# Mixture of experts: rows of 14 experts added behind the last two, all summed in PSUM by identity and one-hot products; the last norm's scale and bias on VectorE

## The chip, the cores and the metric

The kernel runs on one core of a Trainium2 chip, in one launch. Five engines work side by side, each through its own list of instructions: TensorE (PE in the rows, with its weight loads as PEld), VectorE (DVE), ScalarE (ACT), GpSimd (POOL) and SyncE (SP), which here only issues transfers. The metric is device time in microseconds (us), as the median over several runs; a shorter time is better. A trace of one execution gives every instruction's start and length.

## What is computed

A stack of blocks over 512 tokens of 1024 features, in float32. The change is in the mixture of experts, which stands in two layers and is followed each time by a residual and a layer norm:

```python
def moe_ffn(x, w_router, b_router, w_gate, w_up, w_down):
    ...
    _, top_e = lax.top_k(jnp.where(in_grp, biased, NEG), TOP_K)
    w = jnp.take_along_axis(s, top_e, axis=-1)
    w = w / jnp.sum(w, axis=-1, keepdims=True)
    gate = jnp.zeros((n, N_EXPERTS), jnp.float32).at[jnp.arange(n)[:, None], top_e].set(w)
    h = jax.nn.silu(jnp.einsum('nd,edf->nef', xt, w_gate)) * jnp.einsum('nd,edf->nef', xt, w_up)
    h = h * gate[:, :, None].astype(h.dtype)
    return jnp.einsum('nef,efd->nd', h, w_down).reshape(B, S, D)
...
        f = moe_ffn(x, moe_w_router, moe_b_router, moe_w_gate[i], moe_w_up[i], moe_w_down[i])
        x = layer_norm(DN_ALPHA * x + f, ln_g[i, 1], ln_b[i, 1])
```

There are 16 experts, of which each token takes two, with weights that sum to one.

## The kernel before

Tokens lie in four tiles of 128 partitions x 1024 features, `xt[0..3]`. Most products take three passes (`mm3`, L394 to L396): both factors are split into a high and a low half (`split`, L369: a cast on ScalarE, a subtract on VectorE), and the three products of 512 columns are summed in PSUM.

A mixture layer `L0` or `L1` is an object. `route` and `token_weights` find each token's two experts, the slots of each expert's 128 rows (`idx`) and the two weights of each token (`wts`). For expert e, `gather` reads its rows from `xd` in DRAM (an indirect transfer on GpSimd's queue), transposes them on the PE into the PSUM tile `xgt` (L1431) and splits them. `up` makes 24 products into `psh`, then the gated activation; `down` transposes that (`ht`, L1448), makes 12 products into `psy`, copies `psy` to the SBUF (ScalarE, L1456) and scatters the rows to `yd` in DRAM (L1457), two rows for each token. `experts` writes this as a pipeline: the gather of e + 1, `up` of e, `down` of e - 1. Weights come as 1 MB pieces on SP's queue (L334); the queue runs ahead as pages of the SBUF come free.

`overflow` (L1376 to L1421) is a branch for an expert with more than 128 rows; the branch is not taken here. All engines pass through it.

`combine` comes behind it. It loads `yd` in eight pieces of 512 KB (L1487), each held until all 16 scatters have landed, and adds them to `xt`, weighted, on VectorE (`mac`, L1502; in layer 0 one of them on ScalarE and GpSimd, L1499). By tile follow the statistics (L1512, L1513), a root on ScalarE (L1514), Newton steps on VectorE (L428, L430), `normalize` on ScalarE (L1173), and `done`. VectorE's order in this loop is the order of the code; other engines are ordered by the scheduler. In layer 0 `done` is `x4_tile`: transposes into `x4T` (L1654), scale and bias on both engines (L1660, L1662), splits, and 48 products into `n`, 280 columns at a time. In layer 1 it is `finish` (L1978 to L1983): scale and bias (`affine`, L360), on GpSimd for the first tiles, shared by both engines for the last two, and the store of the tile.

## Time and profile before

| | us |
|---|---|
| median of 3 runs | 1924.97 (1920.96 to 1928.03) |
| profiled execution, whole time | 1918.51 |
| its span, first to last instruction | 1916.7 |
| PE busy in the span | 1743.3 (91%) |
| DVE busy | 1221.8 (64%) |
| ACT busy | 874.1 (46%) |
| POOL busy | 173.3 (9%) |
| experts of layer 0, first transposes to last product | 1096.8 to 1255.9 |
| end of layer 0, to the last product of n | 1255.9 to 1318.2 |
| experts of layer 1 | 1706.1 to 1871.8 |
| end of layer 1 | 1871.8 to 1916.7 |

The share of busy time is a mean over stages with different limits. What a stage is worth is read from its own rows: which engine is full there, and which wait ends last.

### The profile page before, as it was taken

The page shows a single profiled execution, that of the slowest core. Times are in us where ns is not written, and L with a number is a line of the kernel's source. Part 1 is how long each engine was busy: PE and PEld are TensorE (multiplying, and loading weights), DVE is VectorE, ACT ScalarE, POOL GpSimd, SP SyncE. Part 2 cuts the span into 40 slices and gives each one's busy share as a digit, 9 for nine tenths or more (in the row PEclk, how much of TensorE's full clock was granted, in tenths as well). Part 3 has the DMA queues.
Part 4 walks back from the last instruction along what each step waited for, and adds up shares of the span by engine and source line. Part 5 has one row for each costly group of instructions (what it writes and reads, how often), then busy time and mean ns, then how long its engine had stood idle before and what let it go on. Part 6 is the DMA issues. An engine that isn't in the chain of part 4 may idle for free.

```text
span 1916.7 us, 27254 instructions
## 1 busy us (share of the span) xinstructions
PE 1743.3 (91%) x10719; PEld 1480.1 (77%) x10719; DVE 1221.8 (64%) x2276; ACT 874.1 (46%) x1397; POOL 173.3 (9%) x140
## 2 busy tenths in 40 slices
PE   8999999899999999999999799949998999859990
PEld 7899877798989988877888578738886777647870
DVE  7855368776555643253347889874337777669985
ACT  4233346433333332243223288843236665628881
POOL 2310000022000000000000122110000000012213
PEclk9999999899999999999999799979898999879995
DMA  5335221242322233212225599752230003539953
GB/s 194 110 110 140 89 88 65 63 160 90 108 89 89 88 135 114 95 66 88 88 88 206 188 325 380 281 217 77 85 136 23 1 12 123 208 126 338 380 224 140
DMA packets 69205, 269.73 MB, mean 141 GB/s; under 512 B 22144, under 2 KB 24720, under 8 KB 44240
## 3 DMA queue, kind: packets, MB, share of 16 engines
q1 hardware_dynamic: 52384, 246.38, 35.9%
q0 software_dynamic: 9216, 16.80, 2.4%
q10 hardware_dynamic: 7472, 4.76, 1.2%
q8 instruction: 85, 1.39, 0.3%
q14 instruction: 48, 0.39, 0.1%
HBM read 249.62 MB, written 30.43 MB: 146 GB/s over the span
## 4 chain that ended last, share of the span: by engine, by line
PE 63%; DVE 6%; ACT 3%; DMA 2%; issue 2%; POOL 0%; SPq 0%; POOLq 0%; DVEq 0%; ACTq 0%
PE mm L396 8%; PE mm L395 8%; PE mm L394 8%; PE psh L395 3%; PE psh L396 3%; PE psh L394 3%; PE tm L394 2%; PE tm L395 2%; PE tm L396 2%; PE npo L1920 2%; PE npt L1908 2%; PE op L395 2%; PE op L394 2%; PE op L396 2%; PE xgt L1431 1%
## 5 line engine op out<-in xcount | busy, mean ns | idle before, releaser
L369 ACT CAST pg<-pg 128x1024 fp32r<-128x1024 f32 (+2 forms) x437 | 427.4, 1007 | 554.1 <-PE mm L395 224.9
L369 DVE TENSOR_TENSOR pg<-pg,pg 128x1024 fp32r<-128x1024 f32 (+2 forms) x437 | 503.0, 1176 | 264.6 <-ACT pg L369 251.4
L396 PE MATMUL mm<-pg,pg 128*128 128x258 f32 (+2 forms) x1504 | 483.0, 322 | 4.0 <-DVE pg L369 4.0
L394 PE MATMUL mm<-pg,pg 128*128 128x258 f32 (+2 forms) x1504 | 484.9, 323 | 1.4 <-ACT pg L888 0.7
L395 PE MATMUL mm<-pg,pg 128*128 128x258 f32 (+2 forms) x1504 | 482.9, 321 | 0.0
L394 PEld LDWEIGHTS mm<-pg,pg 128*128 128x128 f32 x1504 | 287.6, 191 | 28.0 <-ACT pg L886 2.8
L396 PEld LDWEIGHTS mm<-pg,pg 128*128 128x128 f32 x1504 | 286.8, 191 | 24.9 <-DVE pg L369 4.7
L395 PEld LDWEIGHTS mm<-pg,pg 128*128 128x128 f32 x1504 | 287.4, 191 | 21.2 <-issue 0.4
L360 DVE TENSOR_TENSOR pg<-mm,pg 128x256 f32<-128x256 f32 (+3 forms) x138 | 66.2, 510 | 138.8 <-PE mm L396 138.8
L395 PE MATMUL psh<-pg,pg 128*128 128x512 f32 x256 | 106.4, 416 | 2.3 <-DVE pg L369 2.3
L394 PE MATMUL psh<-pg,pg 128*128 128x512 f32 x256 | 101.9, 398 | 0.0
L396 PE MATMUL psh<-pg,pg 128*128 128x512 f32 x256 | 101.3, 396 | 0.0
L394 PE MATMUL tm<-pg,pg 128*128 128x512 f32 x192 | 76.4, 408 | 4.6 <-ACT pg L1145 4.6
L395 PE MATMUL tm<-pg,pg 128*128 128x512 f32 x192 | 77.3, 403 | 1.2 <-DVE pg L369 1.2
L396 PE MATMUL tm<-pg,pg 128*128 128x512 f32 x192 | 76.1, 396 | 0.0
L360 DVE TENSOR_TENSOR pg<-pg,pg 128x512 f32<-128x512 f32 (+12 forms) x103 | 57.1, 575 | 24.9 <-ACT pg L675 10.6
L1892 ACT ACTIVATE pg<-ns,nmx 128x512 f32<-128x512 f32 (+3 forms) x128 | 66.3, 531 | 11.4 <-DVE nmx L1888 7.2
L1888 DVE TENSOR_REDUCE nmx<-ns 128x2 f32<-128x1024 f32 (+3 forms) x48 | 50.1, 1043 | 17.3 <-PE ns L1885 17.1
L360 DVE TENSOR_TENSOR pg<-pg 128x64 f32<-128x64 f32 (+8 forms) x127 | 49.5, 411 | 17.4 <-ACT pg L1033 15.4
L395 PEld LDWEIGHTS psh<-pg,pg 128*128 128x128 f32 x256 | 48.9, 191 | 13.2 <-DVE pg L369 4.4
L1425 POOL DMA_INDIRECT pg<-xd,idx x32 | 38.1, 1189 | 219.2 <-DVE wts L360 122.7
L394 PEld LDWEIGHTS psh<-pg,pg 128*128 128x128 f32 x256 | 48.8, 191 | 11.4
(440 smaller groups left out, 2960.9 us busy)
## 6 DMA issues: line engine op xcount, KB each, us to landing
pg<-in_w_moe_dram SPq DMA_DIRECT2D x96, 1024.0 KB, 10.4
pg<-in_w_up_dram SPq DMA_DIRECT2D x22, 1024.0 KB, 4.8
pg<-in_w_dn_dram SPq DMA_DIRECT2D x11, 1024.0 KB, 4.9
pg<-in_w_g_dram SPq DMA_DIRECT2D x8, 1024.0 KB, 5.5
pg<-in_w_go_dram SPq DMA_DIRECT2D x8, 1024.0 KB, 4.8
pg<-yd SPq DMA_DIRECT2D x16, 512.0 KB, 7.8
pg<-in_w_n_dram SPq DMA_DIRECT2D x8, 1024.0 KB, 6.8
pg<-in_w_no_dram SPq DMA_DIRECT2D x8, 1024.0 KB, 4.8
```

Source lines behind the costliest of these rows:

```text
L360: return (eng or V).tensor_tensor(o, a, b, op=op)
L369: return A.copy(h, src), V.tensor_tensor(l, src, h.bitcast(F32), op=ALU.subtract)
L394: TE.matmul(o, a[0], b[0], start=start, stop=False)
L395: TE.matmul(o, a[0], b[1], start=False, stop=False)
L396: TE.matmul(o, a[1], b[0], start=False, stop=stop)
L1425: ld = G.indirect_dma_start(out=xg, out_offset=None, in_=self.xd, in_offset=bass.IndirectOffsetOnAxis(ap=self.idx[:, e:e + 1], axis=0), bo ...
L1431: TE.transpose(ps[:, k // 4, (k % 4) * P:(k % 4 + 1) * P], xg[:, k * P:(k + 1) * P], ident)
L1888: V.tensor_reduce(mx, sc, axis=AX.X, op=ALU.max, negate=True)
L1892: A.activation(pp[:, r, br], sc[:, r, br], AF.Exp, bias=mx[:, r, br:br + 1], accum_out=se[:, r, br:br + 1])
L1908: TE.transpose(src[:, r, br, c * P:(c + 1) * P], pp[:, r, br, c * P:(c + 1) * P], ident)
L1920: TE.matmul(o_[64 * r:64 * r + 64], vsw[:, c * 512 + br * 256 + g * 64:c * 512 + br * 256 + (g + 1) * 64], pts[r][:, br, c * P:(c + 1) * P ...
```

## The change

Zeros are written once to a small DRAM tile `zd` and copied from there over both layers' `yd` (`zero`, 16 transfers of 512 KB from DRAM to DRAM). The rows of experts 14 and 15 are not scattered any more. ScalarE scales them by their slot's weight as it copies them (`sw`, found in `token_weights` by eight small products), and VectorE writes a one-hot matrix for each of these two experts and each tile (slot against token, `tokf`). `experts` itself loads `yd` when the scatter of expert 13 has landed, in four pieces of 1 MB, and VectorE adds all of them to `xt` ahead of the overflow branch; the branch reloads `xt` and repeats this if it is taken. In `combine` the PE sums three products by tile in PSUM: identity times `xt`, and the one-hots of experts 14 and 15 times their rows (`early`, `last`). The statistics and `normalize` read PSUM. `gather` loses its transposes to `turn`, which stands behind the sixth of eight steps of `up` of the expert before. In the last layer scale and bias are VectorE's, and the last tile goes out in two halves.

```diff
+    zd = dr.tile([P, 1024], F32, tag="zd", name="zd")
+    G.memset(xt[0], 0.0)
+    nc.sync.dma_start(out=zd, in_=xt[0])
...
+            self.tokf = small("tokf", (2,))
+            V.tensor_scalar(self.tokf, psi[:, 14:16], float(2 * S), None, op0=ALU.add)
...
+            w16, tl = small("w16", (2, 4, 3, 2), F16), small("tl", (2, 4, 2))
+            tt(tl, self.oh[:, :, :, 14:], bc(self.wts, 2), ALU.mult)
...
+            for i, (k, t) in enumerate(self.q):
+                TE.matmul(psp[:, :6], self.q[k, t], w16[:, k, t].rearrange("p a e -> p (a e)"), start=i == 0, stop=i == 7)
...
+        def zero(self):
+
+            for i in range(2 * S // P):
+                nc.sync.dma_start(out=self.yd[i * P:(i + 1) * P, :], in_=zd)
+
+        def load(self, t, y):
+            return nc.sync.dma_start(out=v2(y), in_=self.yd.rearrange("(a k) d -> a k d", k=2)[t * P:(t + 1) * P])
+
+        def mac(self, t, y):
+            for k in range(2):
+                V.scalar_tensor_tensor(xt[t], y[:, k * 1024:(k + 1) * 1024], self.wts[:, k, t:t + 1], xt[t], op0=ALU.mult, op1=ALU.add)
...
+        def turn(self, xg, behind=None):
+
             ps = p2("xgt")
             for k in range(KD):
-                TE.transpose(ps[:, k // 4, (k % 4) * P:(k % 4 + 1) * P], xg[:, k * P:(k + 1) * P], ident)
+                i = TE.transpose(ps[:, k // 4, (k % 4) * P:(k % 4 + 1) * P], xg[:, k * P:(k + 1) * P], ident)
+                if behind is not None:
+                    after(i, behind)
...
+            if e < 14:
+                A.copy(v2(yo), psy)
+                s = self.scatter(yo, self.idx[:, 16 + e:17 + e])
...
+            self.last = A.activation(v2(yo), psy, AF.Copy, scale=self.sw[:, e - 14:e - 13]).ins.name
+            m = self.xg[1][:, (e - 14) * 512:(e - 13) * 512]
+            for t in range(4):
+                V.tensor_scalar(m[:, t * P:(t + 1) * P], iota, float(t * P), self.tokf[:, e - 14:e - 13], op0=ALU.add, op1=ALU.is_equal)
+            self.late.append((m, yo))
...
+            xg = {0: self.gather(0)}
+            g, hs = {0: self.turn(xg.pop(0))}, {}
             for e in range(17):
                 if e == 1:
                     wt.behind = None
                 if e < 15:
-                    g[e + 1] = self.gather(e + 1)
+                    xg[e + 1] = self.gather(e + 1)
                 if e < 16:
                     hs[e] = self.up(g.pop(e))
+                if e < 15:
+                    g[e + 1] = self.turn(xg.pop(e + 1), self.upto)
                 if e > 0:
                     self.down(e - 1, hs.pop(e - 1))
-            drop("xg", "gh", "gl", "hs", "hhl", "ysb", "wr", "wh", "wl")
+
+            for t in range(4):
+                y.append(sb(2048, "wr", F32, WM))
+                ld = self.load(t, y[t])
...
+            for t in range(4):
+                self.mac(t, y[t])
...
+            def early(t):
+
+                ps = p2("late")
+                for nh in range(2):
+                    c = slice(nh * 512, (nh + 1) * 512)
+                    TE.matmul(ps[:, nh], ident, xt[t][:, c], start=True, stop=False)
+                    TE.matmul(ps[:, nh], self.late[0][0][:, t * P:(t + 1) * P], self.late[0][1][:, c], start=False, stop=False)
+                return ps
+
+            def last(t):
+                for nh in range(2):
+                    TE.matmul(z[t][:, nh], self.late[1][0][:, t * P:(t + 1) * P], self.late[1][1][:, nh * 512:(nh + 1) * 512], start=False, stop=True)
+
+            z = [early(0), early(1)]
+            last(0)
+            last(1)
...
+                            V.bn_stats(bs[:, 6 * j:6 * j + 6], z[t][:, j])
...
+                        normalize(v2(xt[t]), z[t], rs)
+                    if t in (1, 2):
+                        z.append(early(t + 1))
+                        last(t + 1)
...
     def finish(t):
-        n = (0, 0, 512, 640)[t]
-        for eng, c in ((V, slice(0, n)), (G, slice(n, 1024))):
-            if c.start < c.stop:
-                affine(xt[t][:, c], [g[:, c] for g in L1.gb], eng)
-        nc.sync.dma_start(out=out[t * P:(t + 1) * P, :], in_=xt[t])
-    L1.combine(finish, ())
+        for c in (slice(0, 1024),) if t < 3 else (slice(0, 512), slice(512, 1024)):
+            affine(xt[t][:, c], [g[:, c] for g in L1.gb], V)
+            nc.sync.dma_start(out=out[t * P:(t + 1) * P, c], in_=xt[t][:, c])
+    L1.combine(finish)
```

How the order moves, at three places. First the PE at the start of layer 1's experts, before: `xgt` is a transposed gather, `psh` the first products of expert 0.

```order
L1306 MATMUL inv<-rr,pg_8436 128x32
L1431 MATMUL xgt<-c_ident,pg_132 128x128 x8
L1431 MATMUL xgt<-c_ident,pg_10600 128x128 x8
L1431 MATMUL xgt<-c_ident,pg_7017 128x128 x8
L394 MATMUL psh<-pg_10084,pg_10085 128x512
L395 MATMUL psh<-pg_10084,pg_10085 128x512
L396 MATMUL psh<-pg_10084,pg_10085 128x512
```

And now, at the second gather's transposes, which stand at the end of `psh` of expert 0:

```order
L394 MATMUL psh<-pg_8476,pg_10552 128x512
L395 MATMUL psh<-pg_8476,pg_10552 128x512
L396 MATMUL psh<-pg_8476,pg_10552 128x512
L1474 MATMUL xgt<-c_ident,pg_10672 128x128 x8
L394 MATMUL psh<-pg_10549,pg_10146 128x512
L395 MATMUL psh<-pg_10549,pg_10146 128x512
L1495 MATMUL ht<-c_ident,pg_10817 128x128 x2
```

The transposes of the second and third gather have moved behind products of the expert ahead of them.

Second, VectorE at the end of layer 1's experts, before: the branch of `overflow` (L1376, L1377), with its inner steps, and behind it the additions.

```order
L369 TENSOR_TENSOR pg_13862<-ht,pg_13862 128x256
L1376 TENSOR_LOAD cnti
L1377 COMPARE_AND_BRANCH
L1379 COPY posr<-pos 128x8
L1381 COMPARE_AND_BRANCH
```

```order
L1377 UNCONDITIONAL_BRANCH
L1502 SCALAR_TENSOR_TENSOR pg_7017<-pg_132,wts,pg_7017 128x1024
L1502 SCALAR_TENSOR_TENSOR pg_7017<-pg_7017,wts 128x1024
L1512 BN_STATS bs<-pg_7017 128x6 x2
L1513 BN_AGGR mv<-bs 128x2
L1502 SCALAR_TENSOR_TENSOR pg_132<-pg_7061,wts,pg_132 128x1024
```

And now:

```order
L369 TENSOR_TENSOR pg_11433<-ht,pg_11433 128x256
L1460 SCALAR_TENSOR_TENSOR pg_7017<-pg_92,wts,pg_7017 128x1024 x2
L1460 SCALAR_TENSOR_TENSOR pg_132<-pg_94,wts,pg_132 128x1024 x2
L1460 SCALAR_TENSOR_TENSOR pg_7060<-pg_11460,wts,pg_7060 128x1024 x2
L1460 SCALAR_TENSOR_TENSOR pg_7060<-pg_7094,wts,pg_7060 128x1024 x2
L1395 TENSOR_LOAD cnti
L1396 COMPARE_AND_BRANCH
```

All eight additions have moved ahead of the branch; no addition is left behind it.

Third, the PE behind the branch in layer 0, before: the first tile's transposes `x4T` come first, then the products `n`.

```order
L1377 UNCONDITIONAL_BRANCH
L1654 MATMUL x4T<-c_ident,pg_7017 128x128 x8
L394 MATMUL n_10153<-pg_8465,pg_483 128x280
L1654 MATMUL x4T<-c_ident,pg_132 128x128 x8
L395 MATMUL n_10153<-pg_8450,pg_483 128x280
```

And now, where `late` are the sums in PSUM (L1558 is the identity's product, L1559 and L1564 the one-hots' of experts 14 and 15):

```order
L1559 MATMUL late<-pg_7017,pg_7064 128x512
L1564 MATMUL late<-pg_6402,pg_7064 128x512 x4
L1718 MATMUL x4T<-c_ident,pg_7017 128x128 x8
L394 MATMUL n_10210<-pg_8476,pg_483 128x280
L395 MATMUL n_10210<-pg_8080,pg_483 128x280
L1558 MATMUL late<-pg_7060,c_ident 128x512
L1559 MATMUL late<-pg_7017,pg_7064 128x512
L1558 MATMUL late<-pg_7060,c_ident 128x512
L1559 MATMUL late<-pg_7017,pg_7064 128x512
L1564 MATMUL late<-pg_6402,pg_7064 128x512 x2
L396 MATMUL n_10210<-pg_8476,pg_10145 128x280
```

Twelve products stand ahead of the first transposes (four for each of two tiles and then two for each), and the third tile's six have come in between the first products of `n`; the fourth's stand in the second tile's `n`.

## Rows read from the trace of the kernel before

**Rows 1.** Busy time by stretch: length, engines (x instructions), PE clock, DMA share, GB/s.

```profile
1744.00:1844.00 100.00, 99.49 (x484) 81.73 (x483) 92.69 (x97) 87.02 (x107) 23.57 (x19) 1.00 0.96 370
...
1880.00:1890.00 10.00, 0.00 (x0) 0.00 (x0) 9.20 (x16) 1.83 (x3) 2.04 (x1) 0.50 0.91 345
```

**Rows 2.** VectorE in order of time, layer 1's end: start, length, what; [idle before].

```profile
1880.11 1.28 DVE L1502 SCALAR_TENSOR_TENSOR pg<-pg,wts,pg 128x1024 f32<-128x1024 f32 x1 [11.02 <-DMA pg<-yd]
...
1883.16 1.29 DVE L1512 BATCH_NORM_STATS2 bs<-pg 128x6 f32<-128x512 f32 x2
...
1887.84 1.29 DVE L1512 BATCH_NORM_STATS2 bs<-pg 128x6 f32<-128x512 f32 x2
...
1889.28 2.10 DVE L1502 SCALAR_TENSOR_TENSOR pg<-pg,wts,pg 128x1024 f32<-128x1024 f32 x1
...
1891.54 2.06 DVE L428 SCALAR_TENSOR_TENSOR bs<-lrs,bs 128x1 f32<-128x1 f32 x1
```

**Rows 3.** GpSimd in order of time: expert 13's scatters, and the last norm's end.

```profile
1246.68 1.11 POOL L1457 DMA_INDIRECT yd<-pg,idx  x1 [7.78 <-ACT pg L1456]
...
1862.52 1.11 POOL L1457 DMA_INDIRECT yd<-pg,idx  x1 [7.78 <-ACT pg L1456]
...
1907.07 3.16 POOL L360 TENSOR_TENSOR pg<-pg,pg 128x384 f32<-128x384 f32 x2 [1.75 <-ACT pg L1173]
```

**Rows 4.** Scatters, issue to landing in us: expert 13's in layer 0, layer 1, all.

```profile
yd<-pg,idx POOLq DMA_INDIRECT x1, 3.3
...
yd<-pg,idx POOLq DMA_INDIRECT x1, 6.3
...
yd<-pg,idx POOLq DMA_INDIRECT x32, 8.8
```

**Rows 5.** PE in order of time, layer 0's end.

```profile
1272.57 1.97 PE L1654 MATMUL x4T<-c_ident,pg 128*128 128x128 f32 x8 [16.66 <-ACT pg L1173]
1282.73 0.60 PE L394 MATMUL n<-pg,pg 128*128 128x280 f32 x1 [8.19 <-ACT pg L369]
...
1287.55 0.29 PE L395 MATMUL n<-pg,pg 128*128 128x280 f32 x1
...
1303.35 0.40 PE L394 MATMUL n<-pg,pg 128*128 128x280 f32 x1 [3.17 <-ACT pg L369]
...
1318.22 0.39 PE L394 MATMUL tm<-pg,pg 128*128 128x512 f32 x1
```

**Rows 6.** PE in order of time, around a float32 product of 512 columns (z).

```profile
831.13 1.02 PE L1100 MATMUL z<-pg,pg 128*128 128x512 f32 x2
...
832.23 0.40 PE L395 MATMUL tm<-pg,pg 128*128 128x512 f32 x1
```

**Rows 7.** ScalarE in order of time, layer 1's end.

```profile
1886.64 1.24 ACT L1173 ACTIVATE pg<-pg,lrs 128x1024 f32<-128x1024 f32 x1 [1.62 <-DVE lrs L1520]
```

**Rows 8.** VectorE in order of time, layer 0's end.

```profile
1302.83 0.73 DVE L1662 TENSOR_SCALAR pg<-x4T,lnfm 128x128 f32<-128x128 f32 x2 [1.48 <-ACT pg L1660]
```

**Rows 9.** PE in order of time, the start of both layers' experts.

```profile
1102.39 0.78 PE L394 MATMUL psh<-pg,pg 128*128 128x512 f32 x1
...
1103.27 0.40 PE L396 MATMUL psh<-pg,pg 128*128 128x512 f32 x1
...
1706.14 1.97 PE L1431 MATMUL xgt<-c_ident,pg 128*128 128x128 f32 x8 [5.84 <-DMA pg<-xd,idx]
...
1716.57 0.78 PE L394 MATMUL psh<-pg,pg 128*128 128x512 f32 x1
```

**Rows 10.** VectorE in order of time, the first gather's subtract in layer 0.

```profile
1099.85 1.22 DVE L369 TENSOR_TENSOR pg<-xgt,pg 128x1024 fp32r<-128x1024 f32 x1 [4.12 <-ACT pg L369]
```

**Rows 11.** VectorE in order of time, four one-hots in layer 1's routing.

```profile
1699.17 0.86 DVE L1299 TENSOR_SCALAR pg<-c_iota,pos 128x128 f16<-128x128 f32 x4
```

**Rows 12.** SP's queue in order of time, where the zeros come in.

```profile
794.70 34.46 SPq L334 DMA_DIRECT2D pg<-in_w_gv_dram  x4
```

**Rows 13.** ScalarE in order of time, the first cast of w_gq.

```profile
882.11 1.05 ACT L369 CAST pg<-pg 128x1024 fp32r<-128x1024 f32 x1 [4.46 <-PE tm L396]
```

More of the change, by code (lines that the diff above doesn't have):

```diff
@@ L1438, in up @@
             for k in range(KD):
-                mm3(psh, (g[0][:, k * P:(k + 1) * P], g[1][:, k * P:(k + 1) * P]), wt.next(512), k == 0, k == KD - 1)
+                i = mm3(psh, (g[0][:, k * P:(k + 1) * P], g[1][:, k * P:(k + 1) * P]), wt.next(512), k == 0, k == KD - 1)
+                if k == 5:
+                    self.upto = i.ins.name
             hs = sb(256, "hs", bufs=2)
@@ L1455, in down @@
             yo = sb(1024, "ysb", bufs=3)
-            self.last = A.copy(v2(yo), psy).ins.name
-            s = G.indirect_dma_start(out=self.yd, out_offset=bass.IndirectOffsetOnAxis(ap=self.idx[:, 16 + e:17 + e], axis=0),
-                                     in_=yo, in_offset=None, bounds_check=2 * S - 1, oob_is_err=False)
-            for o in self.scat:
-                tc.declare_no_dep(s.ins, o.ins, reason="rows of another expert's tokens")
-            self.scat.append(s)
+            if e < 14:
+                A.copy(v2(yo), psy)
+                s = self.scatter(yo, self.idx[:, 16 + e:17 + e])
+                for o in self.scat:
+                    tc.declare_no_dep(s.ins, o.ins, reason="rows of another expert's tokens")
+                self.scat.append(s)
+                return
+            self.last = A.activation(v2(yo), psy, AF.Copy, scale=self.sw[:, e - 14:e - 13]).ins.name
[3 more added lines that the diff above has]
+            self.late.append((m, yo))
         def experts(self):
-            drop("zT", "lng", "lnb")
+            drop("zT", "lngb")
             wt.bufs = 4
-            self.scat = []
-            g, hs = {0: self.gather(0)}, {}
+            self.scat, self.late, y = [], [], []
+            xg = {0: self.gather(0)}
+            g, hs = {0: self.turn(xg.pop(0))}, {}
             for e in range(17):
@@ L1491, in combine @@
+            st.behind = ld.ins.name
+            for t in range(4):
+                self.mac(t, y[t])
+            drop("gh", "gl", "hs", "hhl", "wr", "wh", "wl")
+            wt.bufs = 2
+        def combine(self, done):
             self.gb = load_gb(2 * self.l + 1)
-            st.behind = ld.ins.name
             eps = small("epsl", (1,))
             V.memset(eps, LN_EPS / ALPHA ** 2)
-            def mac(t, k):
-                if k == 0 and t in aside:
-                    A.activation(y2[t, 0], y2[t, 0], AF.Copy, scale=self.wts[:, 0, t:t + 1])
-                    tt(xt[t], xt[t], y2[t, 0], ALU.add, G)
-                else:
-                    V.scalar_tensor_tensor(xt[t], y2[t, k], self.wts[:, k, t:t + 1], xt[t], op0=ALU.mult, op1=ALU.add)
+            def early(t):
[11 more added lines that the diff above has]
+            last(1)
@@ L1674, in x4_tile @@
         nc.sync.dma_start(out=kcd[t * P:(t + 1) * P, :], in_=s_)
-    L0.combine(x4_tile, (3,))
+    for _ in range(2):
+        sb(512, "kcv", bufs=2)
+    L0.combine(x4_tile)
     drop("x4f")
```

60 lines of the change are left out of this document (32 added, 28 removed).

## Prediction

> **What bounds the kernel now.** I read four views, in this order. First the busy times by stretch: inside the experts the PE is busy 99.5 of 100 us at full clock, so a mixture layer gains nothing there; what can move is its start and its end, where the PE idles. In the last layer's end the PE does nothing, its clock stands at 0.50, and VectorE is the full engine (9.2 of 10 us) [rows 1]. Second, the order of time on VectorE in that end: the first addition waits 11 us for the load of yd, and then a tile costs 4.7 us while GpSimd is idle (1883.16 to 1887.84); beside GpSimd's scale and bias, an addition of 1.28 us takes 2.10 and a step on a single column 2.06 [rows 2]. Third, GpSimd's and the queues' rows: the scatter of expert 13 starts at 1862.52, 17.6 us before the first addition, since the loads wait for that of expert 15 [rows 2, 3]. Fourth, the PE in the first layer's end: 16.7 us idle before the first transposes, 8.2 before the next norm projection n, 3.2 later, and dense work from there on [rows 5]. So the time ends, in layer 0, when n of the fourth tile is through (1318.22), and in layer 1 with the last store.
>
> **The change part by part.** I call S the landing of expert 13's scatter, M the end of the eight additions, P the start of the first product with the identity.
>
> *End of layer 1.* Expert 13's scatter starts at 1862.52; such scatters land 3.3 to 6.3 us later, so S is 1865.8 to 1868.8, and I take 1867.5 [rows 3, 4]. The four loads are 4.2 MB; at the 345 GB/s of this stretch that is 12.2 us [rows 1], the additions follow as the tiles land, and the last pair is 2.5 us [rows 2]: M = S + 15 = 1882.5. The rows of order show that all eight stand ahead of the branch around the overflow on VectorE, and the PE's first product waits for that branch; so P = 1882.8, not the time of the first tile. The PE has idled since its last expert then and is at 0.50 [rows 1]. A float32 product of 512 columns: z is one, in two records; it starts at 831.13, and the next stream is back at its normal pace at 832.23, whose first step of 0.23 lies before that; so 0.87 us at full clock, 1.74 at half [rows 6]. How long the half clock lasts I take from layer 0, where n began at 0.50 at 1282.73 and ran at the full rate by 1287.5: some 4.4 us [rows 5]. Ten products stand ahead of the first statistics: 2.5 in 4.4 us, 7.5 in 6.5, together 10.9. So the first statistics come at 1893.7, where they now come at 1883.16.
> Then the tiles. Statistics and their sum are 1.5, the steps to the inverse root 0.9 (the 4.7 us of an undisturbed tile, less those 1.5 and two additions of 1.2), its wait for ScalarE's root some 0.3, normalizing 1.24 [rows 2, 7]: the first tile's result leaves PSUM at P + 14.9. There are two such PSUM buffers, so the third tile's six products run from there to P + 20.1, the fourth's to P + 25.3. VectorE then has the fourth statistics (to 26.8), scale and bias of the third tile (two of 1.2, the additions' length: 29.2), Newton (30.1), normalizing on ScalarE (31.4), and four half-width steps of 0.65: P + 34.0. From the last step to the end it is 6.5 us now (GpSimd's end at 1910.2 to 1916.7) [rows 3], less 0.5 allowed for a store of half the size: P + 40 = 1922.8, **+6 us**. What is won from GpSimd (twice 2.7 us of slowed steps) and from the early loads is spent on products at a cold clock and a serial PSUM chain. Bounds: S at its early end and a warm clock -4, -2; the clock falling again in the gap before P + 14.9, and S late, +2, +1.5; with an allowance for waits: 0 to +12.
>
> *End of layer 0.* The same with S = 1250.0 (1246.68 + 3.3) [rows 3, 4]: M 1265, P 1265.5, first statistics 1276.4, first transposes 1280.4, against 1272.57. To the first n it is another 4.6 us: VectorE has the multiply by the scale (1.2), the pair of 0.73, the add and the second pair [rows 8], so n starts at 1285.0 against 1282.73: +2.3. Behind it the PE was 35.5 us at work to 1318.22. Twelve more products lie in that stretch now, 10.4 us; of the waits that they can fill there are 3.17 and the half clock behind it, some 1.7 [rows 5]. I let them fill 4: 2.3 + 10.4 - 4 = 8.7, of which I take **+8** (from +2, all filled and n as early as now, to +13, none filled). What follows is dense PE work, so it is passed on.
>
> *Start of a layer.* In layer 0 the first expert's rows are transposed, cast and subtracted by 1101.1, and psh could start there instead of 1102.39 [rows 9, 10]: -1.3. But the other two gathers' transposes now lie behind psh (2 x 0.87), the second's cast and subtract (1.0 and 1.22, less 0.5 of products that need only the high half) stand open between psh of expert 0 and 1, and the clock, which was full from 1103.3 on because the transposes ran on, is lost for half of another 4.4 us (2.2): -1.3 + 1.7 + 1.7 + 2.2 = 4.3, less 0.7 of waits that were there already; I take **+3** (0 to +5). In layer 1 psh stood behind the third gather until 1716.57; the first transposes end at 1708.1 [rows 9], and with 2.2 for the split and 0.5 allowed for the sw steps ahead of the subtract it moves to 1710.8: -5.8 + 1.7 + 1.7, less 0.7: **-3** (-5 to +1). The clock is at half in both orders there.
>
> *The rest.* Eight one-hots a layer are 0.86 us per four on VectorE [rows 11], which is 93% busy in the experts [rows 1]; ScalarE's copies gain no length: **+1** for both layers (0 to 3.4). The sw products and sums fall in the wait for gathers: 0 (to 1.5). The two scatters less per layer were behind the PE: 0. The zeros are 8.4 MB from DRAM to DRAM, which no row shows. They go between the loads of w_gv and w_gq on SP's queue; w_gv's last issue is at 829.2, w_gq's first cast at 882.1 [rows 12, 13]. With a memset and a store ahead (about 5 us) and w_gq's load behind (about 5), they have 42 us. At the 370 GB/s of the expert loads they take 23, and 46 if each byte counts twice: 0 (to +4); I take 0, since the loads are the nearest row.
>
> Sum: 6 + 8 + 3 - 3 + 1 = **+15 us**. The profiled execution took 1918.5 us (span 1916.7), 6.5 under the median; it would come to 1933.5, the median to **1940**. Half a per cent is 9.6 us, about what a measurement here can tell from no change.
>
> **The rivals.**
> *The products start with the first tile.* If the first product waits only for its own two additions, P is 7.5 us earlier in both layers: the sums at the ends fall to about -1.5 and +0.5, the whole to 0: **1925**, not slower. Against it stands the order of the branch; for it, that the semaphore's count is all that I have. It decides at P: 1875 against 1882.
> *One pass.* If a product of 512 columns costs 0.23 as the experts' do, the first statistics come 6 us sooner and VectorE's 4.8 us a tile becomes the pace: -2 in each end, **1922**. Against it: z's two records [rows 6].
> *Late scatters.* If expert 13's rows land 8.8 us after issue, the median of all scatters [rows 4], S moves by 5.5 in layer 0 and 4 in layer 1: **1949**. Expert 13's own 3.3 and 6.3 speak against it, VectorE's full load for it. The Trainium skill, "SBUF — State Buffer", section "SBUF: two separate sides", states a rule for this: descriptors of GpSimd's transfers can't be written while a VectorE operation holds the port pair that the two share. [...]
> *A cold PE.* If the clock stays at 0.50 in the last norm (the PE waits for buffers), twelve products cost 0.87 more each: **1950**.
> *Zeros in the way.* At 100 GB/s they end near 918, and w_gq is some 40 us late: **1980**. Nothing in the trace speaks for so low a rate.
>
> **How the numbers follow.** Forecast 0.44 (own range 1928 to 1952; 0.10 of it within half a per cent), early start 0.16 (0.12 within, 0.04 faster with the starts at their low ends), one pass 0.08 (0.05 and 0.03), late scatters 0.09 (0.01 within), cold PE 0.09, zeros 0.07, a wait that goes and that I have not priced 0.07 (0.05 faster, 0.02 within). Faster 0.12, within 0.30, slower 0.58. The range 1921 to 1957 leaves out the zeros and most of the faster cases.
>
> **What would show it.** Right: in layer 1 the last addition ends near 1882 and the first product right behind it; records of such products of twice 0.43 us, longer at first; statistics 4.7 to 5.5 us apart; no step of 2 us on VectorE; n of the fourth tile in layer 0 ending some 8 us later against the first transposes of its experts; the PE idle for 2 us behind psh of expert 0. Wrong: a product ahead of the additions' end, tiles closer than 4.7 us, w_gq's first cast waiting for its load, or a PE that is idle in the experts.

## The result and the profile after

The changed kernel takes 1943.64 us (median of 4 runs, 1942.19 to 1946.63), the kernel before in the same comparison 1923.57 (1920.96 to 1928.03). The ratio is 1.0105, with a 95% interval from 1.0084 to 1.0126: slower by 1%, 20 us. Forecast were 1940 us and +15. The direction and the time are as forecast; several terms of the sum are not, and that their misses cancel in part is luck.

Where the time went is read from the PE's own milestones in the two profiled executions (spans 1916.7 and 1941.7): first and last instruction of each stage, one subtracted from the other. (`go` and `op` are products ahead of layer 0's experts, `tm` and `cim` products behind `n`.)

| stage, us | before | after | difference | forecast |
|---|---|---|---|---|
| start to the first `op` products (near 1012) | 1012.2 | 1015.5 | +3.3 | 0 |
| from there to the experts of layer 0 | 84.6 | 85.6 | +1.0 | 0 |
| experts of layer 0, first `xgt` to last `psy` | 159.1 | 163.7 | +4.6 | +3, and half a us of one-hots |
| end of layer 0, last `psy` to the first `cim` | 90.2 | 108.0 | +17.8 | +8 |
| from there to the experts of layer 1 | 360.0 | 361.3 | +1.3 | 0 |
| experts of layer 1 | 165.6 | 161.9 | -3.7 | -3, and half a us of one-hots |
| end of layer 1, last `psy` to the end | 45.0 | 45.7 | +0.7 | +6 |

The sum is +25.0, where the forecast had +15. It is also 5 more than between the medians, which is what the profiled execution of before lies below its own median (1918.51 against 1923.57); the one of after lies on its median. A difference of that size is seen in one stage: layer 0's experts took 159.1 us in that execution, and 164.7 and 165.3 in the two others that have the same order there (below).

Layer 0's end on the PE in order of time (start, length, what, idle before it), to be held against [rows 5]:

```profile
1274.25 2.05 PE L1558 MATMUL late<-pg,c_ident 128*128 128x512 f32 x2 [9.47 <-DVEq L1396]
1276.09 1.91 PE L1559 MATMUL late<-pg,pg 128*128 128x512 f32 x2
...
1281.52 1.02 PE L1559 MATMUL late<-pg,pg 128*128 128x512 f32 x2
...
1291.85 1.97 PE L1718 MATMUL x4T<-c_ident,pg 128*128 128x128 f32 x8 [4.16 <-ACT pg L1177]
...
1297.18 0.60 PE L394 MATMUL n<-pg,pg 128*128 128x280 f32 x1 [3.36 <-ACT pg L369]
...
1297.82 1.91 PE L1558 MATMUL late<-pg,c_ident 128*128 128x512 f32 x2
...
1327.11 0.40 PE L394 MATMUL n<-pg,pg 128*128 128x280 f32 x1 [3.57 <-ACT pg L369]
...
1338.59 0.40 PE L394 MATMUL n<-pg,pg 128*128 128x280 f32 x1 [2.05 <-ACT pg L369]
```

The products wait for VectorE's pass through the branch and start at half clock: a product is two records, and products follow each other 1.71 us apart (1276.09, 1277.80), later, at full clock, 0.86 (1281.52, 1282.38). The first transposes come 27 us after the last expert product, where they came 16.7 after it before, and `n` still waits twice later on.

VectorE in the same stretch:

```profile
1263.89 10.15 DVE L1460 SCALAR_TENSOR_TENSOR pg<-pg,wts,pg 128x1024 f32<-128x1024 f32 x8 [1.75 <-DMA pg<-yd]
...
1285.92 1.91 DVE L369 TENSOR_TENSOR pg<-pg,pg 128x1680 fp32r<-128x1680 f32 x1 [7.12 <-ACT pg L369]
1287.75 1.29 DVE L1574 BATCH_NORM_STATS2 bs<-late 128x6 f32<-128x512 f32 x2
```

All eight additions in one piece, done at 1274.04; M was to be S + 15, and `yd`'s loads were issued at 1259.23: 14.8. Then something that the prediction did not have: the first statistics stand behind a subtract of a piece of `w_n1`, whose cast waits for its transfer.

Layer 1's end on VectorE, to be held against [rows 2]:

```profile
1894.94 5.12 DVE L1460 SCALAR_TENSOR_TENSOR pg<-pg,wts,pg 128x1024 f32<-128x1024 f32 x4 [1.57 <-DMA pg<-yd]
1901.26 5.12 DVE L1460 SCALAR_TENSOR_TENSOR pg<-pg,wts,pg 128x1024 f32<-128x1024 f32 x4 [1.20 <-SPq L1396]
1917.92 1.29 DVE L1574 BATCH_NORM_STATS2 bs<-late 128x6 f32<-128x512 f32 x2 [11.54 <-PE late L1564]
...
1920.59 1.29 DVE L1574 BATCH_NORM_STATS2 bs<-late 128x6 f32<-128x512 f32 x2
...
1925.18 1.29 DVE L1574 BATCH_NORM_STATS2 bs<-late 128x6 f32<-128x512 f32 x2
...
1929.94 1.29 DVE L1574 BATCH_NORM_STATS2 bs<-late 128x6 f32<-128x512 f32 x2
...
1935.92 2.74 DVE L360 TENSOR_TENSOR pg<-pg,pg 128x512 f32<-128x512 f32 x4 [1.33 <-ACT pg L1177]
```

The eight additions end at 1906.38, 10.3 us after the last expert product; VectorE then has nothing to do for 11.5 us. The second tile's statistics follow the first's by 2.7 us, the next ones by 4.6 and 4.8, and no step of 2 us on a single column is left; GpSimd does nothing here.

The PE at the same place, and its granted clock there (columns: length; busy us of PE, PEld, VectorE, ScalarE, GpSimd with instructions; clock; DMA share; GB/s):

```profile
1906.59 2.04 PE L1558 MATMUL late<-pg,c_ident 128*128 128x512 f32 x2 [10.56 <-DVEq L1396]
...
1911.71 1.02 PE L1559 MATMUL late<-pg,pg 128*128 128x512 f32 x2
...
1916.00 3.60 PE L1564 MATMUL late<-pg 128*128 128x512 f32 x8
1919.43 1.02 PE L1558 MATMUL late<-pg,c_ident 128*128 128x512 f32 x2
```

```profile
1905.00:1910.00 5.00, 3.41 (x4) 1.50 (x5) 1.34 (x2) 0.00 (x0) 0.00 (x0) 0.50 0.02 7
1910.00:1915.00 5.00, 5.00 (x11) 2.19 (x10) 0.00 (x0) 0.00 (x0) 0.00 (x0) 0.84 0.00 0
```

Last, a difference that has nothing to do with the change. Between 1000 and 1016 us, where both kernels run the same products, the PE of the changed kernel was busy without a gap at half clock:

```profile
1000.00:1016.00 16.00, 16.00 (x71) 14.95 (x71) 7.35 (x20) 2.22 (x3) 2.41 (x3) 0.51 0.00 1
```

The same stretch of before stands at 1.00. The stage from `go` to `op`, in which it lies, takes 26.08 us here and 19.39 to 19.40 in the profiled executions of before and of all experiments below: 6.7 us in one execution of 14, taken as chance here. (The table's first row has +3.3 and not +6.7, since the first `go` came 3.4 us sooner in after; it lies between 986.5 and 994.1 in the 14 executions.)

### The profile page after: what moved, and what is told of

The parts are those of the page before. It is cut to its first block, busy times and chain, and to the rows that moved or that the text cites. A ratio compares the mean times of both kernels' runs of the same rounds, so it can differ in the third digit from the quotient of the medians.

```text
span 1941.7 us, 27485 instructions
## 1 busy us (share of the span) xinstructions
PE 1796.7 (93%) x10831; PEld 1503.2 (77%) x10831; DVE 1225.0 (63%) x2315; ACT 877.2 (45%) x1396; POOL 145.8 (8%) x128
## 3 DMA queue, kind: packets, MB, share of 16 engines
q1 hardware_dynamic: 52032, 255.30, 36.6%
## 5 line engine op out<-in xcount | busy, mean ns | idle before, releaser
L360 DVE TENSOR_TENSOR pg<-pg,pg 128x512 f32<-128x512 f32 (+11 forms) x109 | 61.5, 584 | 36.9 <-PE x4T L1718 12.4
L1958 ACT ACTIVATE pg<-ns,nmx 128x512 f32<-128x512 f32 (+3 forms) x128 | 66.2, 529 | 10.4 <-DVE nmx L1954 6.0
L394 PEld LDWEIGHTS psh<-pg,pg 128*128 128x128 f32 x256 | 49.3, 193 | 17.4 <-ACT pg L369 7.3
L395 PEld LDWEIGHTS psh<-pg,pg 128*128 128x128 f32 x256 | 49.3, 193 | 13.4 <-DVE pg L369 3.2
L396 PEld LDWEIGHTS psh<-pg,pg 128*128 128x128 f32 x256 | 49.3, 192 | 13.0 <-DVE pg L369 2.8
```

Source lines behind the costliest of these rows:

```text
L360: return (eng or V).tensor_tensor(o, a, b, op=op)
L394: TE.matmul(o, a[0], b[0], start=start, stop=False)
L395: TE.matmul(o, a[0], b[1], start=False, stop=False)
L396: return TE.matmul(o, a[1], b[0], start=False, stop=stop)
L1958: A.activation(pp[:, r, br], sc[:, r, br], AF.Exp, bias=mx[:, r, br:br + 1], accum_out=se[:, r, br:br + 1])
```

## Experiments

The theory after the result: the loss lies in layer 0's end alone; it is made by products that stand between the additions and the statistics on a PE that has gone cold, and by further products in a stretch where the PE sets the time. Layer 1's end pays the same products, but gets their price back from VectorE. The rivals are those of the prediction and the start of the layers.

### One layer's end undone at a time

In `l0_old` layer 0 is as before from its scatters on (all 16 scattered, `combine` as it was), and its zeros and the steps for `sw` are left out too; layer 1 is as changed. In `l1_old` it is the reverse. `turn` keeps its new place in both.

```diff
-    L0.combine(x4_tile)
+    L0.combine_old(x4_tile, (3,))
```

> Layer 0 as before the change from its scatters on (16 scatters, eight loads behind the last one, additions and statistics as before), with the new place of the transposes; layer 1 as changed. Theory: the loss lies in layer 0's end, where the traces show 17.7 us more from the last expert product to the stream behind n; it should go, so some 1926 us, and the end of layer 0 as long as before (90 us from the last psy to cim). Rival: the ends are neutral and the loss lies ahead of them (a stretch of products at half clock near 1000 us, the starts of the experts): then 1941 to 1944, with the end of layer 0 no shorter than 16 us less.

> Layer 1 as before the change from its scatters on, GpSimd sharing scale and bias; layer 0 as changed. Theory: in layer 1 the late first statistics (10 us) and the faster tiles and end (10 us) cancel, so the time stays at 1943, within 2 us. Rival: taking GpSimd out of the last norm is a gain by itself that the products only partly eat: then putting it back costs 4 us or more, 1948. A third possibility, that layer 1's end is a loss: under 1940.

`l0_old`: 1917.9 us, ratio 0.9978 (0.9960 to 0.9996). Its milestones are those of before in layer 0's end (89.2 us against 90.2 before and 108.0 after), and layer 1's end is 44.9. So the whole loss is gone, and a small gain is left. `l1_old`: 1940.78, ratio 1.0084 (1.0064 to 1.0104), with layer 0's end at 108.0 and layer 1's at 44.3: undoing layer 1 takes 1.4 us off its end, and the interval of the ratio overlaps that of the changed kernel (1.0084 to 1.0126). The loss lies in layer 0's end; layer 1's end is neutral to within some 1.5 us.

### The transposes in their old place

```diff
-                    xg[e + 1] = self.gather(e + 1)
+                    g[e + 1] = self.turn(self.gather(e + 1))
...
-                if e < 15:
-                    g[e + 1] = self.turn(xg.pop(e + 1), self.upto)
```

> Only the transposes of a gather go back to their place ahead of the products of the expert before. Theory: in layer 0 the stretch from the first transposes to the last expert product gets 4 to 5 us shorter (no open split between psh of expert 0 and 1, clock up earlier), in layer 1 it gets 3 us longer (third gather waited for): 1942 in all. Rival: the place of the transposes sets the pace of every expert: then both layers move the same way by over 5 us, 1933 or 1953.

1948.78 us, ratio 1.0124 (1.0106 to 1.0142): not shorter but, if anything, longer. The experts take 165.3 us in layer 0 and 166.7 in layer 1, against 163.7 and 161.9 with the new place. The PE at layer 0's start shows why the forecast for layer 0 was wrong:

```profile
1104.52 1.97 PE L1474 MATMUL xgt<-c_ident,pg 128*128 128x128 f32 x8 [4.57 <-DMA pg<-xd,idx]
1106.14 0.78 PE L394 MATMUL psh<-pg,pg 128*128 128x512 f32 x1
```

The third gather's rows come 4.6 us late and hold the first products, as they did in layer 1 before, 10.4 us behind the first transposes there [rows 9]. In the profiled execution of before they happened to be on time in layer 0, and `psh` began 5.6 us after the first transposes. That was taken for the rule. The last gathers of both layers before, layer 0's with the second one in one line:

```profile
1098.95 3.80 PE L1431 MATMUL xgt<-c_ident,pg 128*128 128x128 f32 x16 [0.18 <-DMA pg<-xd,idx]
...
1714.95 1.97 PE L1431 MATMUL xgt<-c_ident,pg 128*128 128x128 f32 x8 [4.51 <-DMA pg<-xd,idx]
```

### The zeros alone

The kernel before, with `zd` and the 16 copies at the place where the change has them.

```diff
+            for i in range(2 * S // P):
+                nc.sync.dma_start(out=self.yd[i * P:(i + 1) * P, :], in_=zd)
```

> The kernel before, with the cleared tile and the 16 copies of zeros added at the place where the change has them, and nothing else. Theory: the copies are hidden; the time is that of before, within 3 us, and the first product with w_gq starts as before. Rival: the copies shift the work of the mixer behind them so that its short products run at half clock near 1000 us, as in the changed kernel: 7 us more, 1930, with a granted clock of 0.5 between 1000 and 1016 us. If half clock shows there in this run and not in others, it is chance and not the copies.

1925.05 us, ratio 0.9999 (0.9986 to 1.0013): hidden. In the changed kernel SyncE issues the 16 copies from 831.75 to 848.1, and the queues are full from 840 to 860 (columns as above):

```profile
820.00:840.00 20.00, 19.66 (x96) 13.66 (x94) 8.96 (x14) 5.24 (x6) 1.42 (x2) 1.00 0.58 207
840.00:860.00 20.00, 17.03 (x73) 13.24 (x71) 11.82 (x15) 14.02 (x10) 0.53 (x1) 1.00 0.97 309
860.00:880.00 20.00, 17.24 (x66) 13.91 (x67) 5.99 (x9) 8.15 (x8) 0.00 (x0) 0.83 0.40 141
```

The start stage of this run (993.2 us up to the first `go`) is that of before (992.8). In the same run the third gather of layer 0 waits 4.4 us and the experts take 164.7: the 159.1 of before's profiled execution is the exception.

### The weight piece ahead of the statistics

`a_wn` is the changed kernel with the piece of `w_n1` that is loaded last split behind the first tile's `x4T` and used last in `n`; the loads of scale and bias go behind it.

```diff
+        if i == 0:
+            mid, st.mark = raw, st.lds[st.used - 1]
...
+        if t == 0:
+            split(mid, *w1[0])
...
-        for k in range(KD):
+        for k in (3, 4, 5, 6, 7, 0, 1, 2):
```

> The changed kernel, with three moves in layer 0's end alone: the piece of w_n1 that is loaded last is split behind the first tile's x4T work and used last in n, and the loads of the norm's scale and bias stand behind it on SP's queue. Theory: the first statistics of layer 0 were held 2.7 us by that split (the products for them had ended at 1285.0, the statistics began at 1287.75); they now follow the products, and from the last psy to cim it is 2.7 us less, 105. Rival: the products behind n set that stretch whatever the statistics do; then 108 stays.

1938.49 us, ratio 1.0066 (1.0045 to 1.0087). VectorE's first statistics now follow the products:

```profile
1281.47 1.29 DVE L1578 BATCH_NORM_STATS2 bs<-late 128x6 f32<-128x512 f32 x2 [7.22 <-PE late L1568]
```

That is 11.7 us behind the first product (1269.77) instead of 13.5, and layer 0's end is 105.6 us instead of 108.0: 1.8 of the 2.4 us at this step of the chain.

### A PE that is kept busy

`warm` lets the PE multiply the identity with itself behind the last expert, 36 products of 128 columns, while the additions run.

```diff
+            ps = p1("warm")
+            for _ in range(36):
+                after(TE.matmul(ps[:, :P], ident, ident, start=True, stop=True), self.fin)
```

> The changed kernel, with 36 idle products (identity by identity, 128 columns, into a PSUM tile that nobody reads) behind the last expert's, in both layers, so that the PE is busy for 8 of the 10 us before its first sum. Theory: the half clock at the start of the sums costs 2.2 us on the path. In layer 1 the first statistics come 2.2 us sooner after the last addition (8.7 instead of 11.3) and the end is 43.5 instead of 45.7; in layer 0 nothing is gained, because the split of w_n1 holds the statistics there. In all 1941. Rival: the clock is not on the path: 45.7 stays. If the clock is at 0.50 all the same, such products don't keep it up.

1940.47 us, ratio 1.0075 (1.0053 to 1.0096). The clock in layer 1's end is full (compare the two rows of after):

```profile
1905.00:1910.00 5.00, 3.92 (x23) 2.80 (x23) 2.84 (x3) 0.00 (x0) 0.00 (x0) 1.00 0.50 185
1910.00:1915.00 5.00, 5.00 (x13) 2.16 (x12) 0.00 (x0) 0.00 (x0) 0.00 (x0) 1.00 0.00 0
```

From the first product to the first statistics it takes 8.9 us (1908.08 to 1916.94) instead of 11.3, and layer 1's end 41.8 instead of 45.7. So the cold clock is worth 2.5 us of the 11.3, and the ten products at full clock are the rest, 8.9. Another 1.4 us of the shorter end are not the clock's: here VectorE's eight additions run without a wait, where they waited 1.2 us in their middle in the changed kernel, and the first product follows the last expert product by 9.1 us instead of 10.6. In layer 0 nothing comes of it (108.3 us): there the weight piece holds the first statistics to 1284.72 all the same, 13.5 us behind the first product.

### Without the identity

`v_add` has the PE sum only the two one-hot products of a tile, and VectorE adds that sum to `xt`. `v_add2` is `v_add` with the moves of `a_wn`. In both, and in the three kernels at the end of this section, the third and fourth tile's products also stand one tile earlier in the code.

```diff
-                    TE.matmul(ps[:, nh], ident, xt[t][:, c], start=True, stop=False)
...
+                        tt(v2(xt[t]), v2(xt[t]), z[t], ALU.add)
```

> The changed kernel without the identity's products: the PE sums only the two one-hot products, which need no addition to be done first, and VectorE adds that sum to xt (one 1024-wide step more for each tile). Theory: the loss is the path from the last addition through ten products at a cold clock, and twelve products behind n. Then in layer 1 the first statistics come some 8 us sooner and the end gets 6 to 8 us shorter (38 instead of 45.7); in layer 0 the stretch from the last psy to cim gets 10 us shorter by the products alone (98), with the first statistics still held by the split of w_n1. In all 1926. Rival: VectorE and the loads set the ends and the products lie beside them: then four more steps of 1.2 us a layer make it 1948.

> v_add with the three moves of a_wn. Theory: the first statistics of layer 0 follow the last addition by one step of 1.2 us; from the last psy to x4T some 15 us instead of 27, to cim some 84 instead of 108; layer 1 as in v_add; in all 1912. Rival: PE work behind n keeps the stretch at 98 as in v_add, since transposes and splits of the next tiles come no sooner: 1926.

`v_add`: 1925.65 us, ratio 0.9994 (0.9980 to 1.0009). By the medians that is 18 us less than the changed kernel, with one product in three gone. The two ends give 12.6 of them (102.0 us instead of 108.0 in layer 0, 39.0 instead of 45.7 in layer 1); the rest lies in neither end, so that the whole came out at the 1926 expected is partly luck. The PE and VectorE of `v_add` in layer 1's end:

```profile
1887.37 3.70 PE L1558 MATMUL late<-pg,pg 128*128 128x512 f32 x8 [1.20 <-ACTq L1396]
1890.91 3.60 PE L1563 MATMUL late<-pg 128*128 128x512 f32 x8
```

```profile
1891.33 5.12 DVE L1460 SCALAR_TENSOR_TENSOR pg<-pg,wts,pg 128x1024 f32<-128x1024 f32 x4 [1.27 <-SPq L1396]
1896.67 1.22 DVE L360 TENSOR_TENSOR pg<-pg,late 128x1024 f32<-128x1024 f32 x1 [0.21 <-DVEq L1396]
1897.92 1.29 DVE L1574 BATCH_NORM_STATS2 bs<-pg 128x6 f32<-128x512 f32 x2
```

The one-hot products need neither `xt` nor the branch's part on VectorE: the PE begins them 1.2 us behind its last expert product, at full clock (1.00 from 1890 to 1900), while VectorE still adds. The sum stands ready when VectorE wants it, and the first statistics come 1.5 us behind the additions instead of 11.5. The end is 39.0 us.

`v_add2` was expected at 1912 and took 1925.61, ratio 1.0004 (0.9985 to 1.0023), as its rival had it. Layer 0's end goes from 102.0 to 98.8 us, but not to the 90.2 of before. Up to the first `n` it is as short as before (26.6 us against 26.8); what is left over lies between the first `n` and the first `cim`: 63.4 us before, 72.2 here. The PE is busy 6.9 us longer in it (with the last tile's four one-hot products, mostly at half clock, and 1.6 us more for the `tm` products) and idles 5.7 us against 3.8: that is the 8.8. The PE is busy 92% of this stretch, and what it is given there is passed on. This last part, about half of layer 0's 17.8 us, is read from the rows: no run takes the one-hot products out of that stretch, or puts the identity last in layer 0.

### The additions behind the branch

The rival of the early start: the eight additions come behind the overflow branch, so that the first product waits for the first tile's pair alone.

```diff
-            for t in range(4):
-                self.mac(t, y[t])
...
+            with tc.manual_schedule(engines={mybir.EngineType.DVE}):
+                for t in range(4):
+                    self.mac(t, self.y[t])
```

> The changed kernel with the eight additions moved behind the overflow branch (the loads stay ahead of it; the branch, if taken, loads yd again). If the price of the late start is what the rival of the early start says, the first products come 7.5 us sooner in each layer and the whole falls to about 1929. If SyncE's part of the branch holds everyone until all loads have landed (in the changed kernel VectorE waits for it 1.2 us between its additions, at 1901.26, and in layer 0 the last load lands at 1270.2), VectorE can't begin before that: the first product comes at 1902.5 to 1904 in layer 1 against 1906.59, at 1272.5 to 1273 in layer 0 against 1274.25, the second and later tiles are held by additions, and the whole is 1937 to 1944. I hold to the second.

1947.98 us, ratio 1.0114 (1.0093 to 1.0135). In layer 0 the pages of three tiles hold pieces of `w_n1` by then, so that the additions wait for those and add them. So layer 0 says nothing, nor does the whole time; layer 1 is read alone, whose pages nothing else takes. There VectorE and the PE show:

```profile
1904.89 10.15 DVE L1457 SCALAR_TENSOR_TENSOR pg<-pg,wts,pg 128x1024 f32<-128x1024 f32 x8 [12.68 <-SPq L1396]
...
1907.64 2.05 PE L1555 MATMUL late<-pg,c_ident 128*128 128x512 f32 x2 [12.79 <-DVE pg L1457]
```

The product does wait for the first pair only, as the rival has it. But the first addition comes 10.0 us behind the last expert product (1894.85), about when the last one ends in the changed kernel (10.3). Two things lie in this. VectorE begins 5.3 us after the first tile's rows have landed (issued at 1891.90, 7.7 us to landing), in a wait that the profile puts down to SyncE's part of the branch. And the loads of `yd` stand behind those of scale and bias here and are issued 3.0 us later against the last expert product than in the changed kernel. The first product comes 12.8 us behind it instead of 10.6, and the end takes 49.1 us. I had expected a gain of 3 to 4 at the first product, which was wrong too. The early start is not to be had by this edit; since the loads moved with it, the run does not show what the early start would be worth alone (12.8 less 3.0 would be 9.8, an estimate).

### Layer 0 undone, three forms of layer 1's end

`best` is `l0_old` with `v_add`'s end in layer 1. `best2` has VectorE add for the first two tiles only. `best3` has VectorE add no sum: three products by tile as in the changed kernel, but with the identity's last.

```diff
-                    TE.matmul(ps[:, nh], ident, xt[t][:, c], start=True, stop=False)
-                    TE.matmul(ps[:, nh], self.late[0][0][:, t * P:(t + 1) * P], self.late[0][1][:, c], start=False, stop=False)
+                        TE.matmul(ps[:, nh], self.late[i][0][:, t * P:(t + 1) * P], self.late[i][1][:, nh * 512:(nh + 1) * 512], start=i == 0, stop=False)
...
-                    TE.matmul(z[t][:, nh], self.late[1][0][:, t * P:(t + 1) * P], self.late[1][1][:, nh * 512:(nh + 1) * 512], start=False, stop=True)
+                    TE.matmul(z[t][:, nh], ident, xt[t][:, nh * 512:(nh + 1) * 512], start=False, stop=True)
```

> Layer 0 from its scatters on as before the change; in layer 1 no identity products: the PE sums the two one-hot products and VectorE adds the sum to xt. My theory: the two findings add, since they lie 600 us apart. Layer 0 as in the run with layer 0 alone undone (1917.9 median), layer 1's end 39.0 us from the last product of the experts instead of 45.0: 1912, ratio 0.994 to 0.996. Rival: what the run without identity products gained lay in layer 0 and in chance; then 1918, ratio 0.998.

> As the run best, but the third and fourth tile of layer 1 are summed in PSUM with the identity again; only the first two are VectorE's. My theory: in the run without identity products VectorE is full from the first sum on (9.6 of 10 us) and the PE is done by 1901.6, 4.8 us before the third tile is wanted; two sums of 1.22 leave VectorE and the four identity products (3.5 us) fit in that time. The end is 36.6 us instead of 39.0, the whole 1909.5, ratio 0.993. Rival: identity products are dear wherever they stand, since they wait for the last addition; then the third tile is late by 2 to 4 us and the whole is 1912 to 1916.

> Layer 0 from its scatters on as before the change. In layer 1 all sums stay in PSUM as in the changed kernel, only with the identity product last in each sum instead of first, so that the one-hot products, which need nothing of VectorE, can run while the additions do. My theory: the changed kernel's end of layer 1 is long because ten products at a falling clock stand between the last addition and the first statistics (13 us from 1905.1 to 1917.9); with the identity last two products stand there, some 1.7 to 2.5 us, and VectorE has no sums to make: the end is 34 to 35.5 us from the last product of the experts (45.7 in the changed kernel, 38.4 in best), the whole about 1909, ratio 0.992. Rival: identity products are dear because they wait for VectorE whatever their place (their weights and the clock fall while the PE waits); then the first statistics come 5 us or more behind the last addition and the end is 38 us or longer.

| | median us | ratio to before | end of layer 1, us |
|---|---|---|---|
| changed kernel | 1943.64 | 1.0105 (1.0084 to 1.0126) | 45.7 |
| `best` | 1912.33 | 0.9931 (0.9918 to 0.9945) | 38.4 |
| `best2` | 1914.40 | 0.9943 (0.9929 to 0.9956) | 36.0 |
| `best3` | 1912.22 | 0.9959 (0.9942 to 0.9975) | 35.6 |

All three are faster than both kernels, by 0.4 to 0.7% against before. The ends are about as expected (39.0, 36.6, 34 to 35.5). The whole times are 0 to 5 us above the expectation, and the three can't be told apart: runs of `best3` reach from 1907.8 to 1919.2, more than their ends differ. So the 1914.4 of `best2` lies in its rival's range, but the rival's mechanism isn't seen: the third tile's sum ends at 1887.7 and is wanted at 1892.1. Against `l0_old` the end of `best3` is 9.3 us shorter (35.6 against 44.9), but the intervals of the two ratios overlap (0.9942 to 0.9975, 0.9960 to 0.9996): the gain of the order is seen in the stage, not clearly in the whole time.

`best3` settles why layer 1's first statistics were late. VectorE and the PE in its layer 1's end:

```profile
1876.44 7.64 DVE L1467 SCALAR_TENSOR_TENSOR pg<-pg,wts,pg 128x1024 f32<-128x1024 f32 x6 [0.37 <-DMA pg<-yd]
...
1884.19 3.70 PE L1622 MATMUL late<-pg,c_ident 128*128 128x512 f32 x8 [1.16 <-DVEq L1403]
1886.21 1.30 DVE L1632 BATCH_NORM_STATS2 bs<-late 128x6 f32<-128x512 f32 x2 [2.13 <-PE late L1622]
```

The same twelve products for the first two tiles, in another order: the eight one-hot products have run by 1883, and between the last addition (1884.1) and the first statistics there are 2.1 us, where there were 11.5. (The 13 us from 1905.1 in the expectation take the seventh addition's end for the last one's, which is 1906.38.) So 9.4 us of the changed kernel's last norm are the place of the identity in the sum, the 2.5 us of the cold clock among them, since here the PE pauses 1.2 us and not 10.6.

## Why the prediction was right, and where not

*End of layer 1, forecast +6, measured +0.7.* The chain up to the products has the order that was forecast: `yd`'s loads are issued 3.7 us behind expert 13's scatter (forecast 5.0), the additions end 16.3 us after that (1890.10 to 1906.38; forecast 15), so that two misses of 1.3 us cancel; the first product follows VectorE's branch, at half clock, and ten products take 11.3 us to the first statistics (forecast 10.9). Against the last expert product the first statistics come 21.9 us behind, where 21.9 were forecast (1893.7 less 1871.8). Two later terms were too dear. The prediction counted two PSUM buffers and had the third tile's products wait for the first's; the rows show them at 1919.43, right behind the second tile's and before any normalizing, so there are at least three, and the last step ends 20.7 us behind the first statistics instead of 23.1. And from there to the end it is 3.0 us (1938.7 to 1941.7) instead of 6.0. Together that is 5.4, all of what the term was off (5.3). One of the signs of being wrong did come, tiles closer than 4.7 us: the first two are 2.7 us apart, as both sums stood ready and no scale and bias lay between them.

*End of layer 0, forecast +8, measured +17.8.* The bound of +13 did not hold either. `n` begins 32.4 us behind the last expert product instead of 26.8: +5.6, where +2.3 was forecast. Of the 3.3 missing, 1.8 are the piece of `w_n1` ahead of the statistics (the ten products end at 1285.98, the statistics start at 1287.75); the rest is ten products in 11.7 us instead of 10.9, and 5.3 us from the transposes to `n` instead of 4.6. In `a_wn`, without that piece, `n` begins 1.4 us sooner. The prediction looked at VectorE's additions and norms there, and not at the weight splits that stand in the same queue. From `n` on it is +12.2, where 6.4 was forecast: twelve products (10.4), of which 4 us were to fall into waits. None did: the PE is busy 10.1 us longer in this stretch and idles 2.1 us more (6.0 against 3.8). The third tile's products run right behind the first of `n`, while the clock is still at half, so they warm the PE instead of filling a gap. The waits of 3.57 and 2.05 us stand later, where no product is left.

*Start of a layer, forecast +3 and -3.* Layer 1 is right: the experts take 161.7 to 164.2 us in the eleven profiled executions with the new place in layer 1, and 165.6 to 166.7 in the three with the old. Layer 0 is not: 161.5 to 164.6 in the same eleven with the new place, and 159.1, 164.7 and 165.3 with the old. The 159.1 is the one execution that the prediction was read from. In this stage the forecast rested on a transfer that came on time by chance: the +4.6 of the table looks like the +3, but against the two other executions with the old place nothing is lost. The forecast then added 6.5 us to go from the profiled execution to the median; this one transfer is worth 5.6 to 6.2 of such a difference.

*One-hots, weights of the tokens, zeros.* Nothing of them is seen: the experts of layer 1 are shorter by 3.7 us with the one-hots in, and the zeros alone make 0.9999. The copies were to run at the 370 GB/s of the nearest rows, the loads; the fullest window above has 309.

*The rivals.* One pass: a float32 product of 512 columns is two records and 0.86 us at full clock, not 0.23. Late scatters: expert 13's rows were there 4.1 and 3.7 us after issue, as the loads of `yd` tell that wait for them; the rule of the Trainium skill ("SBUF — State Buffer", section "SBUF: two separate sides") about GpSimd's descriptors is stated for VectorE operations in a two-port mode, and whether the subtractions that ran beside these two scatters are such, no run here shows. Cold PE: full pace came back 5.1 us behind the first product in layer 1 and stayed, as forecast; in layer 0 it came back after 6.4 us and was lost again while the PE waited for the first transposes, which the forecast did not have. Early start: the first product came at 1906.59, 0.2 us behind the last addition, so it did not start with the first tile; what an early start would be worth is open (`mac_behind`). Zeros: hidden (`b_zeros`).

*What is not explained.* The medians differ by 20 us; without the 6.7 us of the chance clock the profiled execution of after would lie near 1937, below all four runs. What the other three lost isn't seen, since each has only a time and a mean clock. By stages the profiled executions account for some 14 us (+17.8 and +0.7 at the ends, -3.7 in layer 1's experts, -1.3 in layer 0's against the two executions with a late gather); the other 6 us between the medians have no place. That the loss lies in layer 0's end is shown by `l0_old`; of its 17.8 us there, `v_add` takes away 6.0 (the identity), `v_add2` 3.2 more (the weight piece), and 8.6 are read from the rows alone.

## What to carry to other kernels

A sum in PSUM is a queue: put what is ready first and what comes late last, and the products run in the shade of what they wait for; the same products put 11.5 us between the last addition and the first statistics in one order and 2.1 in the other. A product that replaces a vector step must be priced at the place where it stands: behind an idle PE it cost double here (1.71 us instead of 0.86), and in the stretch behind `n`, where the PE was busy 92% of the time, 10.1 us more of products made the stretch 12.2 us longer. Before a term is read from one execution, look whether the same wait appears in the sister stage; if it is there in one and not in the other, it may be chance.

## What was not expected of the hardware

- The granted clock fell from 1.00 to 0.50 near 1000 us and stayed there to 1016, behind some 20 us in which the PE had been busy without a gap at full clock (narrow float32 products of the scan at the last), in one execution and in none of the 13 others. It cost 6.7 us.
- At layer 0's start two executions with the same order of work differ in how long the half clock lasts: over the first 20 us of the experts the mean clock is 0.67 in `v_add` and 0.84 in `v_add2`, and the experts take 164.6 and 161.7 us.
- A branch that is not taken costs each engine its own time: the PE passed layer 1's 1.2 us behind its last product when nothing behind it needed VectorE, while VectorE stood idle for 12.7 us in `mac_behind`, which the profile puts down to SyncE's part.
